# Sixteen of 44 weight cases of a down projection in a seven-product 2x2 scheme

## The chip, the cores and the metric

The kernel runs on one core of one Trainium2 chip. The metric is the device time of one execution, in microseconds (us), as the median of several runs. The engines are named as in the profile: PE is TensorE, DVE is VectorE, ACT is ScalarE, POOL is GpSimd, SP is the queue from which most transfers (DMAs) are issued.

## The reference

Two decoder layers over 256 tokens with a model width of 2048, each a mixer and a gated feed-forward network (FFN) with a causal convolution of width 3, and a final RMSNorm. The change concerns the second layer's FFN and the norm behind it.

```python
D_MODEL = 2048; SEQ = 256; DEPTH = 2; D_FF = 5632; CONV_W = 3; EPS = 1e-6

def conv_ffn(h, w_up, cw, cb, w_down):
    S = h.shape[1]
    a = h @ w_up                                   # 2048 -> 2 * 5632
    ap = jnp.pad(a, ((0, 0), (CONV_W - 1, 0), (0, 0)))
    c = sum(ap[:, k:k + S] * cw[k] for k in range(CONV_W)) + cb
    gate, val = c[..., :D_FF], c[..., D_FF:]
    return (jax.nn.silu(gate) * val) @ w_down      # 5632 -> 2048

def reference(x, mem, positions, ...):
    for l in range(DEPTH):
        ...
        x = x + jnp.concatenate([main, mo], axis=-1) @ w_out[l]
        x = x + conv_ffn(rmsnorm(x, g_ffn[l]), w_up[l], conv_w[l], conv_b[l], w_down[l])
    return rmsnorm(x, g_final)
```

## The kernel before

All data is fp32, and a product of fp32 accuracy is made of three matmuls. Each operand is split into a high part, which TensorE takes exactly, and the rest: `whi` is ACT's copy of a raw weight tile into the matmul's type, `wlo` is DVE's subtraction raw − `whi`. A product is then high × high + high × low + low × high. A raw tile is 128 x 1024 numbers (512 KB). There are four buffers for raw tiles, four for `whi` and five for `wlo`, so the loads and the splits run ahead of TensorE until one of these is used up.

The FFN takes the 5632 hidden columns in three parts of 4, 4 and 3 groups of 512 (`FF_GROUPS`). For each part there is an up stage: for each group a GEMM for the gate (`eg`) and one for the value (`ev`), both `gemm_fm`, feature-major, with matmuls of 256 columns; their results go through the convolution (`conv`: one operation on ACT, three on DVE), the gate through Silu, and gate times value, again split in two, lands in `h`. Then comes the part's down stage. In the first layer it is `gemm_fm` too. In the second layer it is token-major (`gemm_tm`, `mm_tm`): for each of four blocks j of 512 output columns, all blocks of 128 hidden columns (k blocks) of the part are multiplied for both blocks of 128 tokens (tb 0 and 1), with matmuls of 512 columns. The sum of a (j, tb) is one PSUM bank, which DVE adds to `xt`, the residual in token-major order (L1146).

In the last part the function `tokens` does the final norm beside it: for each (j, tb) ACT squares and sums (L1158), for j below 3 DVE multiplies by `gb`, the gain spread over the partitions (L1162), at j = 2 the three sums are reduced (L1165, L1166), and at j = 3 the scalar steps L1171 to L1178, the output scaling on ACT (L1182) and DVE (L1183, L1184) and the output transfers follow. `late=4` in the last j means that its last four chunks are done for tb 0 first and for tb 1 afterwards, the last chunk of tb 1 in two halves of 256 columns, and the order of PE, DVE and ACT is there as written. `gb` is loaded before this FFN.

Elsewhere a scheduler orders each engine's instructions, by its own estimates; `manual_schedule` fixes the written order within its scope.

Of the kernel before, what the change touches and what calls it, by code (L numbers as in the profile page):

```python
# [30 lines left out]
THETA = 10000.0  # L31
EPS = 1e-6
FF_GROUPS = (4, 4, 3)


def exact_pieces(value, bits, count):
# [33 lines left out]
class Kernel:  # L70
# [359 lines left out]

    def start(self):
        nc, t, tc = self.nc, self.t, self.tc
        self.x = self.ap.tile([P, NB, S], F32, name="xT")
        self.xhl = self.halves()
        mhl = self.ap.tile([P, NB, 512], F32R, tag="big", name=self.uid("memhl"))
        self.kT = [pool.tile([P, MH, S], F32, name=self.uid("kT")) for pool in (self.mk, self.cp)]
        self.mv = [pool.tile([P, 2, MW], F32, name=self.uid("mv")) for pool in (self.mk, self.cp)]
# [156 lines left out]
    def three(self, o, w, x, start, stop):  # L594
        mm, (wh, wl), (xh, xl) = self.nc.tensor.matmul, w, x
        mm(o, wh, xh, start=start, stop=False)  # L596
        mm(o, wh, xl, start=False, stop=False)  # L597
        mm(o, wl, xh, start=False, stop=stop)  # L598

    def memory_split(self, l, h, q, keys, rest):  # L600
        i, v = h % 2, self.mv[l][:, :, h * P : (h + 1) * P]
# [88 lines left out]
                done()  # L690


    def ffn(self, l, after=None, to_tokens=None, tokens=None):
        nc, t = self.nc, self.t
        rb = self.tmp(self.cp, [P, S], "rbc", 2)
# [3 lines left out]
        with self.tc.tile_pool(name=self.uid("ff"), bufs=1) as fp:  # L699
            g0 = 0  # L700
            for part, ng in enumerate(FF_GROUPS):
                h = self.ap.tile([P, NB, 512], F32R, tag="big", name=self.uid("h"))

                def conv(b, acc):
                    a = self.scaled(self.tmp(fp, [P, S], "a", 2), acc, rb)
# [4 lines left out]
                    nc.vector.scalar_tensor_tensor(c[:, 2:], a[:, : S - 2], w(0), c[:, 2:], ALU.mult, ALU.add)  # L710
                    return c

                for g in range(g0, g0 + ng):
                    gate = self.tmp(fp, [P, 4, S], "gate", 2)

                    def eg(b, acc):
                        c = conv(4 * g + b, acc)
                        nc.scalar.activation(gate[:, b, :], c, AF.Silu)

                    def ev(b, acc):  # L720
                        c = conv(FB + 4 * g + b, acc)
                        hv = self.tmp(fp, [P, S], "hv", 2)
                        nc.vector.tensor_tensor(hv, gate[:, b, :], c, ALU.mult)
                        self.split(h[:, 4 * (g - g0) + b, :], hv)

                    ks = list(range(NB))
                    turns = to_tokens if to_tokens is not None and g == 1 else {}
                    self.gemm_fm(self.rows(up, g * 512, 512), ks, 4, lambda k: xhl[k], eg, hooks=first if g == 0 else {})
                    self.gemm_fm(self.rows(up, FF + g * 512, 512), ks, 4, lambda k: xhl[k], ev, hooks=turns)
                last = part == len(FF_GROUPS) - 1  # L730
                if last and l == 0:
                    self.new_hl()
                dn = down[g0 * 512 : (g0 + ng) * 512]
                for j in range(4):
# [12 lines left out]
                    self.gemm_fm(src, list(range(4 * ng)), 4, lambda k: h[:, k, :], ed)  # L747
                g0 += ng


    def x_rstd(self):
# [363 lines left out]
    def run(self):  # L1115
        nc, tc, t = self.nc, self.tc, self.t
        self.constants()
        with tc.tile_pool(name="mk", bufs=1) as self.mk:
            self.start()
            self.layer_a()  # L1120
        self.ffn(0, lambda j: self.next_operand(j, None))
        self.layer_b()
        with tc.tile_pool(name="fin", bufs=1) as fin:

            xt = fin.tile([P, 2, D], F32, name="xt")
            gb = fin.tile([P, D], F32, name="gb")
            sums = fin.tile([P, 2, 5], F32, name="fsums")
            part = fin.tile([P, 2], F32, name="fpart")
            r = fin.tile([P, 2], F32, name="froot")
            q = fin.tile([P, 2], F32, name="fq")  # L1130
            v = fin.tile([P, 2], F32, name="fv")
            nc.sync.dma_start(out=gb, in_=t["g_final"].rearrange("(o d) -> o d", o=1).to_broadcast([P, D]))

            def turn(r):
                xs = self.tmp(fin, [P, 2, NB, 32], "xs", 2)
                ins = nc.vector.transpose(out=xs, in_=self.x.rearrange("p k (a r j) -> p a k r j", a=2, j=32)[:, :, :, r, :])
                tc.keep_in_program_order(ins)
                o = xt[32 * r : 32 * (r + 1)].rearrange("j a (k q i) -> j q (a k) i", q=4, i=32)
                for q in range(4):
                    nc.sync.dma_start(out=o[:, q], in_=xs[32 * q : 32 * (q + 1)].rearrange("j a k i -> j (a k) i"))  # L1140

            def tokens(j, tb, acc, last, half=None):
                c0, n = (0, 512) if half is None else (256 * half, 256)
                c = slice(j * 512 + c0, j * 512 + c0 + n)
                o = xt[:, tb, c]
                add = lambda o, a: nc.vector.tensor_tensor(o, a, o, ALU.add)  # L1146
                add(o, acc[:, c0 : c0 + n])
                if not last:
                    return
                junk = self.tmp(fin, [P, 512], "fjunk", 2)  # L1150
                one = lambda x: x[:, tb : tb + 1]
                if half == 1:

                    nc.vector.tensor_tensor_reduce(
                        out=junk[:, :n], in0=o, in1=o, scale=-0.5 / D, scalar=one(part), op0=ALU.mult, op1=ALU.add, accum_out=one(v)
                    )
                else:
                    nc.scalar.activation(junk[:, :n], o, AF.Square, accum_out=sums[:, tb, j : j + 1])  # L1158
                if half == 0:
                    add(xt[:, tb, j * 512 + 256 : (j + 1) * 512], acc[:, 256:])  # L1160
                if j < 3:
                    nc.vector.tensor_tensor(o, o, gb[:, c], ALU.mult)  # L1162
                if j == 2:

                    nc.vector.tensor_reduce(one(part), sums[:, tb, 0:3], AX.X, ALU.add)  # L1165
                    nc.vector.tensor_scalar(one(part), one(part), -0.5 / D, -0.5 * EPS, ALU.mult, ALU.add)  # L1166
                    nc.scalar.activation(one(r), one(part), AF.Sqrt, scale=-2.0)
                if j == 3:
                    if half != 1:
                        total = one(part) if half == 0 else one(v)  # L1170
                        nc.vector.tensor_scalar(total, sums[:, tb, 3:4], -0.5 / D, one(part), ALU.mult, ALU.add)  # L1171
                    if half == 0:
                        return

                    nc.scalar.activation(one(r), one(v), AF.Sqrt, scale=-2.0)
                    nc.vector.reciprocal(one(r), one(r))
                    nc.vector.scalar_tensor_tensor(one(q), one(r), one(r), one(v), ALU.mult, ALU.mult)
                    nc.vector.scalar_tensor_tensor(one(r), one(q), 1.5, one(r), ALU.add, ALU.mult)  # L1178

                    y, rows = xt[:, tb, :], slice(tb * P, (tb + 1) * P)  # L1180
                    for a in (0, 1024):
                        nc.scalar.activation(y[:, a : a + 512], y[:, a : a + 512], AF.Copy, scale=one(r))  # L1182
                    nc.vector.tensor_scalar(y[:, 512:1024], y[:, 512:1024], one(r), None, ALU.mult)  # L1183
                    nc.vector.scalar_tensor_tensor(y[:, 1536:], y[:, 1536:], one(r), gb[:, 1536:], ALU.mult, ALU.mult)  # L1184
                    nc.sync.dma_start(out=self.out[0, rows, :1024], in_=y[:, :1024])
                    (nc.scalar if tb else nc.sync).dma_start(out=self.out[0, rows, 1024:], in_=y[:, 1024:])

            turns = {2 * r: [lambda r=r: turn(r)] for r in range(4)}
            self.ffn(1, to_tokens=turns, tokens=tokens)


INV_FREQ = [float(1.0 / (THETA ** (2.0 * i / ROPE))) for i in range(HALF)]
# [23 lines left out]
```

## Time and profile before

| | |
|---|---|
| median of 3 runs | 2051.38 us (2051.24 to 2051.41) |
| the profiled execution | 2050.37 us, span 2048.6 us, granted clock 0.999 |
| PE busy | 2038.7 us, 16274 instructions |
| DVE busy | 1411.5 us, 2138 instructions |
| ACT busy | 1079.5 us, 1565 instructions |
| second layer's down stages | 1496.4 to 1583.4, 1757.6 to 1844.5 and 1975.2 to 2040.5 us |
| tail | 2040.5 to 2048.6 us |

The span is what the profiler records between the first and the last instruction; 1.8 us of the profiled execution's time lie around it. Busy times are sums over listed durations. Matmuls are pipelined, so the listed time of one is longer than the distance between two. In the rows that follow, "x" counts instructions, "<-" stands between an output and its inputs, and square brackets hold the idle time before an instruction and what ended it. In the windows table PEclk is the granted TensorE clock as a share of full speed and the number behind it the busy share of the DMA engines.

### The profile page before, as it was taken

The numbers are of one execution on the slowest core, as the hardware profiler recorded it, in microseconds if no ns is written. First come the engines' busy times: TensorE is split into PE (matmuls) and PEld (weight loads), VectorE is DVE, ScalarE is ACT, GpSimd is POOL, SyncE is SP. The second block draws the span as 40 slices with busy tenths as digits, with TensorE's granted clock in tenths as the row PEclk, the third lists the DMA queues.
The fourth block names the chain that finished last, engine by engine and source line by source line (L and its number), as shares of the span: only waits on it lengthen the run. The fifth ranks groups of instructions, "written<-read, shape, count | busy, mean of one in ns | idle before, by whom it ended". The sixth has DMA issues, their size and how long they took to land.

```text
span 2048.6 us, 39833 instructions
## 1 busy us (share of the span) xinstructions
PE 2038.7 (100%) x16274; PEld 1972.0 (96%) x16274; DVE 1411.5 (69%) x2138; ACT 1079.5 (53%) x1565; POOL 142.5 (7%) x200
## 2 busy tenths in 40 slices
PE   9999999999999999999999999999999999999998
PEld 8989999999999999999999999999988999889996
DVE  6866767767656766557788786777765667646765
ACT  6754744555435555345555575455543555435554
POOL 0000013000000000000043241400000000000000
PEclk9999999999999999999999999999999999999999
DMA  8776566666666666666665635568666666666664
GB/s 252 233 216 182 165 195 189 194 195 195 195 193 190 196 195 195 195 193 191 196 195 176 186 121 175 184 201 232 198 192 191 198 193 195 193 191 194 198 182 154
DMA packets 244796, 394.66 MB, mean 193 GB/s; under 512 B 53823, under 2 KB 61317, under 8 KB 244485
## 3 DMA queue, kind: packets, MB, share of 16 engines
q1 hardware_dynamic: 244420, 391.58, 64.2%
q8 instruction: 127, 2.08, 0.4%
q10 hardware_dynamic: 192, 0.54, 0.1%
q14 instruction: 57, 0.46, 0.1%
HBM read 387.88 MB, written 2.10 MB: 190 GB/s over the span
## 4 chain that ended last, share of the span: by engine, by line
PE 99%; ACT 0%; DVE 0%; DMA 0%; issue 0%; ACTq 0%
PE ps L152 26%; PE ps L153 26%; PE ps L155 26%; PE ps L184 6%; PE ps L185 6%; PE ps L186 6%; PE ps L518 1%; PE ps L597 0%; PE ps L598 0%; PE ps L596 0%; PE ps L1025 0%; PE ps L814 0%; PE ps L401 0%; PE ps L1053 0%; PE ps L639 0%; DMA graw<-in_g_mem 0%
## 5 line engine op out<-in xcount | busy, mean ns | idle before, releaser
L114 DVE TENSOR_TENSOR wlo<-raw,whi 128x1024 fp32r<-128x1024 f32 x660 | 818.4, 1243 | 517.4 <-ACT whi L113 511.5
L113 ACT ACTIVATE whi<-raw 128x1024 fp32r<-128x1024 f32 x660 | 700.4, 1062 | 845.1 <-PE ps L153 620.2
L152 PE MATMUL ps<-xhl,whi 128*128 128x256 f32 x3264 | 762.7, 277 | 0.0
L153 PE MATMUL ps<-xhl,whi 128*128 128x256 f32 x3264 | 761.0, 276 | 0.0
L153 PEld LDWEIGHTS ps<-xhl,whi 128*128 128x128 f32 x3264 | 612.7, 188 | 0.3
L152 PEld LDWEIGHTS ps<-xhl,whi 128*128 128x128 f32 x3264 | 612.7, 188 | 0.3
L155 PE MATMUL ps<-xhl,wlo 128*128 128x256 f32 x3264 | 436.5, 276 | 0.0
L155 PEld LDWEIGHTS ps<-xhl,wlo 128*128 128x128 f32 x3264 | 400.3, 188 | 0.0
L152 PE MATMUL ps<-h,whi 128*128 128x256 f32 x704 | 163.6, 276 | 0.0
L153 PE MATMUL ps<-h,whi 128*128 128x256 f32 x704 | 163.6, 276 | 0.0
L185 PE MATMUL ps<-wlo,h 128*128 128x512 f32 x354 | 137.2, 388 | 0.0
L184 PE MATMUL ps<-whi,h 128*128 128x512 f32 x354 | 136.8, 388 | 0.0
L186 PE MATMUL ps<-whi,h 128*128 128x512 f32 x354 | 136.8, 388 | 0.0
L153 PEld LDWEIGHTS ps<-h,whi 128*128 128x128 f32 x704 | 131.9, 188 | 0.0
L152 PEld LDWEIGHTS ps<-h,whi 128*128 128x128 f32 x704 | 131.8, 188 | 0.0
L152 PE MATMUL ps<-mainhl,whi 128*128 128x256 f32 x512 | 119.6, 277 | 0.0
L153 PE MATMUL ps<-mainhl,whi 128*128 128x256 f32 x512 | 119.3, 276 | 0.0
L708 ACT ACTIVATE c<-a,cT 128x256 f32<-128x256 f32 x176 | 99.3, 589 | 0.4 <-DVE a L232 0.3
L153 PEld LDWEIGHTS ps<-mainhl,whi 128*128 128x128 f32 x512 | 96.0, 188 | 0.0
L152 PEld LDWEIGHTS ps<-mainhl,whi 128*128 128x128 f32 x512 | 95.9, 188 | 0.0
L155 PE MATMUL ps<-h,wlo 128*128 128x256 f32 x704 | 94.1, 276 | 0.0
L232 DVE TENSOR_TENSOR a<-ps,rbc 128x256 f32<-128x256 f32 x176 | 69.9, 418 | 25.0 <-PE ps L155 24.9
(316 smaller groups left out, 2251.3 us busy)
## 6 DMA issues: line engine op xcount, KB each, us to landing
raw<-in_w_ffn_up SPq DMA_DIRECT2D x352, 512.0 KB, 4.3
raw<-in_w_ffn_down SPq DMA_DIRECT2D x176, 512.0 KB, 4.6
raw<-in_w_out SPq DMA_DIRECT2D x64, 512.0 KB, 4.5
raw<-in_w_in_a SPq DMA_DIRECT2D x56, 512.0 KB, 4.2
raw<-in_w_mem_kv SPq DMA_DIRECT2D x31, 512.0 KB, 4.3
raw<-in_w_in_b SPq DMA_DIRECT2D x16, 512.0 KB, 4.3
raw<-in_w_kv_a SPq DMA_DIRECT2D x9, 512.0 KB, 5.0
raw<-in_w_uq SPq DMA_DIRECT2D x12, 384.0 KB, 3.1
```

Of the source, the lines that this page charges most:

```text
L113: nc.scalar.activation(hi[:, :n], raw[:, :n], AF.Copy)
L114: nc.vector.tensor_tensor(lo[:, :n], raw[:, :n], hi[:, :n].bitcast(F32), ALU.subtract)
L152: mm(acc[:, :S], wh, x[:, :S], start=first, stop=False)
L153: mm(acc[:, :S], wh, x[:, S:], start=False, stop=False)
L155: mm(acc[:, :S], wl, x[:, :S], start=False, stop=last)
L184: mm(acc, xh, wh, start=first, stop=False)
L185: mm(acc, xh, wl, start=False, stop=False)
L186: mm(acc, xl, wh, start=False, stop=last)
L232: self.nc.vector.tensor_tensor(out, acc[:, :S], r, ALU.mult)
L518: nc.tensor.matmul(acc[:, :S], w[:, o : o + P], x, start=k == 0 and n == 0, stop=k == NB - 1 and n == 2)
L708: nc.scalar.activation(c, a, AF.Identity, scale=w(2), bias=w(3))
```

## The change

Only the second layer's down stages and the final norm are changed in substance. A part's down stage now has two phases of 1024 output columns each. A phase goes over pairs of k blocks; one pair by one phase is a case, two k blocks by two column blocks. There are 22 pairs, so 44 cases. A plain case is what it was: per token block and column block two products, 24 matmuls of 512 columns. A fast case sees the tokens (2 blocks) by k (2 blocks) times k by columns (2 blocks) as a 2x2 by 2x2 product and uses seven products in place of eight, 21 matmuls. Which pairs are fast, and the order of pairs in a phase, is in the table `FF_FAST`: three of eight pairs in the parts of four groups, two of six in the last, in both phases: 6 + 6 + 4 = 16 cases.

The right-hand sums of a fast case come from DVE in `fast_pair`: four sums of 512 columns (`xs`), and the splits of `y`, `x`'s left half (`we`), `t13` and `t24`: three `whi`/`wlo` of 1024 and one of 512. The left-hand sums are made once per pair in `ev` (`quarters`, tile `src`), by DVE, split on ACT and DVE.

A phase uses eight PSUM banks: `e00`, `e01`, `e10`, `e11` for the four output blocks, and `m1`, `m5`, `m6`, `m7` for products that more than one output needs. After the phase's last fast case `between` copies the four m banks to `staged` on ACT, and `combine` adds them to `xt` in six DVE operations. In the first two parts `combine` is put into the next part's first gate GEMM (`deferred`). In the last part the first phase's runs at the eviction of `e00`, the second's right after `between`. The evictions and the norm are now in `Tokens.evict`. The last phase has `late=2`: of its last two cases tb 1 is left to the end.

`gb` is now loaded at the start of the last part's down stage, into the SBUF of half of the FFN's input (tag `xhl0`), and `staged` into that of the residual. The raw loads of a down stage are 128 rows of 1024 columns in place of two blocks of 512. Hidden blocks that do not fit into `h` beside the sums go to other tiles (`place`). `three` swaps its second and third matmul. In `Tokens.evict` the output of columns 0 to 1023 is sent in two pieces.

```diff
 FF_GROUPS = (4, 4, 3)
+FF_FAST = {
+    4: ((2, 3, 4), ((0, 1, 2, 5, 3, 6, 4, 7), (2, 0, 3, 1, 4, 5, 6, 7))),
+    3: ((1, 2), ((0, 1, 3, 2, 4, 5), (1, 0, 2, 3, 4, 5))),
+}
...
+    def fast_pair(self, raws, pool):
...
+        b21, b22 = parts(y)
+        one = self.tmp(pool, [P, 1040], "we", 1, F32R)[:, :1024]
+        nc.scalar.activation(one[:, left], x[:, left], AF.Copy)
+        tt(one[:, right], x[:, left], one[:, left].bitcast(F32), ALU.subtract)
+        b11 = one[:, left], one[:, right]
+        t13, t24 = sums
+        tt(t13[:, left], x[:, left], x[:, right], ALU.add)
+        tt(t13[:, right], x[:, right], y[:, right], ALU.add)
+        t1, t3 = parts(t13)
+        tt(t24[:, left], t13[:, left], y[:, right], ALU.add)
+        tt(t24[:, right], t24[:, left], y[:, left], ALU.add)
+        t2, t4 = parts(t24)
+        return b21, b22, b11, t1, t3, t4, t2
...
+    def down_phase(self, dn, col, order, fast, lhs, rhs, pool, between, evict, late=0):
...
+            if k in fast:
+                names7 = "e00", "e01", "m1", "m5", "m7", "e10", "m6"
+                for name, q, w in zip(names7, (1, 6, 0, 4, 3, 2, 5), self.fast_pair(raws, pool)):
+                    three(name, rhs(k, q), w)
+                if k == last_fast:
+                    between([acc[m] for m in names[0]])
...
+        with self.tc.manual_schedule(engines={ET.PE, ET.DVE, ET.Activation}):
+            for half in range(2):
+                evict(0, half, acc[f"e0{half}"])
+            for k, ws in kept:
+                plain(k, ws, 1, 0)
+            evict(1, 0, acc["e10"])
...
-                    if tokens is not None:
-                        self.gemm_tm(
-                            src, 4 * ng, 512, lambda k: h[:, k, :], lambda tb, acc, i=None: tokens(j, tb, acc, last, i), late=4 if last and j == 3 else 0
-                        )
-                        continue
...
+    def between(self, accs):
+        for i, acc in enumerate(accs):
+            self.nc.scalar.activation(self.staged[:, self.ph, i, :], acc, AF.Copy)
+        if self.last and self.ph:
+            self.combine(1)
+        else:
+            self.waiting.append(self.ph)
+
+    def combine(self, ph):
+        xt, m = self.xt, self.staged[:, ph]
...
+        tt(m[:, 2], m[:, 2], m[:, 0], ALU.subtract)
+        tt(m[:, 3], m[:, 3], m[:, 2], ALU.add)
+        tt(xt[:, 0, n1], xt[:, 0, n1], m[:, 0], ALU.add)
+        tt(xt[:, 1, n1], xt[:, 1, n1], m[:, 3], ALU.subtract)
+        tt(xt[:, :, n2], xt[:, :, n2], m[:, 1:2].to_broadcast([P, 2, 512]), ALU.add)
+        tt(xt[:, :, n2], xt[:, :, n2], m[:, 2:4], ALU.add)
```

The order of instructions shows two places. The first is DVE in the last part's down stage, where one set of output columns is finished and the next begun. Before, two banks (`ps_23953`, `ps_23954`) are evicted between splits:

```order
L114 TENSOR_TENSOR wlo_24093<-raw_24091,whi_24092 128x1024
L114 TENSOR_TENSOR wlo_24111<-raw_24109,whi_24110 128x1024
L1146 TENSOR_TENSOR xt<-ps_23953,xt 128x512
L1146 TENSOR_TENSOR xt<-ps_23954,xt 128x512
L114 TENSOR_TENSOR wlo_24129<-raw_24127,whi_24128 128x1024
L1162 TENSOR_TENSOR xt<-xt,gb 128x512 x2
L114 TENSOR_TENSOR wlo_24147<-raw_24145,whi_24146 128x1024
```

Now, from the first eviction (`e00` of the first phase, `ps_24020`) to the third (L1359 is the eviction, L1340 `combine`, L725 to L729 the sums of the second fast case, L703 and L716 splits):

```order
L1359 TENSOR_TENSOR xt<-ps_24020,xt 128x512
L1340 TENSOR_TENSOR staged_24017<-staged_24017 128x512
L725 TENSOR_TENSOR xs_24384<-raw_24380 128x512
L716 TENSOR_TENSOR wlo_24320<-xs_24303,whi_24319 128x1024
L1340 TENSOR_TENSOR staged_24017<-staged_24017 128x512
L1340 TENSOR_TENSOR xt<-xt,staged_24017 128x512
L726 TENSOR_TENSOR xs_24384<-raw_24380,raw_24382 128x512
L703 TENSOR_TENSOR wlo_24349<-raw_24344,whi_24348 128x1024
L728 TENSOR_TENSOR xs_24385<-xs_24384,raw_24382 128x512
L722 TENSOR_TENSOR we_24390<-raw_24380,we_24390 128x512
L1340 TENSOR_TENSOR xt<-xt,staged_24017 128x512
L1340 TENSOR_TENSOR xt<-xt,staged_24017 128x2x512
```

Between the first and the next eviction there now stand the first phase's `combine`, two splits and the sums of the second fast case; the evictions of the other three banks follow after three more splits.

The second place is DVE at the end of the program. Before, tb 0's last block (`ps_24195`) is finished up to its scaling, then come the two halves of tb 1's (`ps_24196`, `ps_24328`):

```order
L1146 TENSOR_TENSOR xt<-ps_24195,xt 128x512
L1171 TENSOR_SCALAR fv<-fsums,fpart 128x1
L1176 RECIPROCAL froot<-froot 128x1
L1177 SCALAR_TENSOR_TENSOR fq<-froot,fv 128x1
L1178 SCALAR_TENSOR_TENSOR froot<-fq,froot 128x1
L1183 TENSOR_SCALAR xt<-xt,froot 128x512
L1184 SCALAR_TENSOR_TENSOR xt<-xt,froot,gb 128x512
L1146 TENSOR_TENSOR xt<-ps_24196,xt 128x256 x2
L1171 TENSOR_SCALAR fpart<-fsums,fpart 128x1
L1146 TENSOR_TENSOR xt<-ps_24328,xt 128x256
```

Now `e00` (`ps_24294`) and `e01` (`ps_24295`) stand there for tb 0, and `e10` (`ps_24296`) for tb 1:

```order
L1359 TENSOR_TENSOR xt<-ps_24294,xt 128x512
L1379 TENSOR_TENSOR xt<-xt,gb 128x512
L1381 TENSOR_REDUCE fpart<-fsums 128x1
L1382 TENSOR_SCALAR fpart<-fpart 128x1
L1359 TENSOR_TENSOR xt<-ps_24295,xt 128x512
L1387 TENSOR_SCALAR fv<-fsums,fpart 128x1
L1391 RECIPROCAL froot<-froot 128x1
L1392 SCALAR_TENSOR_TENSOR fq<-froot,fv 128x1
L1393 SCALAR_TENSOR_TENSOR froot<-fq,froot 128x1
L1397 TENSOR_SCALAR xt<-xt,froot 128x512
L1398 SCALAR_TENSOR_TENSOR xt<-xt,froot,gb 128x512
L1359 TENSOR_TENSOR xt<-ps_24296,xt 128x512
```

and after these `e10`'s own steps, before `e11` (`ps_24297`, and `ps_24569` for its last quarter):

```order
L1379 TENSOR_TENSOR xt<-xt,gb 128x512
L1381 TENSOR_REDUCE fpart<-fsums 128x1
L1382 TENSOR_SCALAR fpart<-fpart 128x1
L1359 TENSOR_TENSOR xt<-ps_24297,xt 128x256 x2
L1387 TENSOR_SCALAR fpart<-fsums,fpart 128x1
L1359 TENSOR_TENSOR xt<-ps_24569,xt 128x256
```

The block of columns 1024 to 1535 is thus finished together with the last block, for both tb, and no longer a block earlier. On ACT the same happens with the squares, and the load of the table for the square root stands between the two of tb 0:

```order
L1375 ACTIVATE fjunk_24523,fsums<-xt 128x512
L1383 ACT_TABLE_LOAD
L1383 ACTIVATE froot<-fpart 128x1
L1375 ACTIVATE fjunk_24530,fsums<-xt 128x512
L1390 ACTIVATE froot<-fv 128x1
L1396 ACTIVATE xt<-xt,froot 128x512 x2
```

It moves from beside the splits, where it is before, to behind the first Square of the end.

More of the change, by code (lines that the diff above doesn't have):

```diff
@@ L690, in w_out, with plain_pair, parts @@
                 done()
+    def plain_pair(self, raws):
+        nc, out = self.nc, []
+        for raw in raws:
+            hi, lo = self.split_tile("whi", True), self.split_tile("wlo", True)
+            nc.scalar.activation(hi, raw, AF.Copy)
+            nc.vector.tensor_tensor(lo, raw, hi.bitcast(F32), ALU.subtract)
+            out.append((hi, lo))
+        return out
+    def fast_pair(self, raws, pool):
+        nc, tt = self.nc, self.nc.vector.tensor_tensor
+        left, right = slice(0, 512), slice(512, 1024)
+        x, y = raws
+        sums = [self.tmp(pool, [P, 1024], "xs", 2) for _ in range(2)]
+        def parts(w):
+            hi, lo = self.split_tile("whi", True), self.split_tile("wlo", True)
+            nc.scalar.activation(hi, w, AF.Copy)
+            tt(lo, w, hi.bitcast(F32), ALU.subtract)
+            return [(hi[:, c], lo[:, c]) for c in (left, right)]
+        b21, b22 = parts(y)
[11 more added lines that the diff above has]
+        return b21, b22, b11, t1, t3, t4, t2
@@ L729, in ffn @@
-                    self.gemm_fm(self.rows(up, FF + g * 512, 512), ks, 4, lambda k: xhl[k], ev, hooks=turns)
-                last = part == len(FF_GROUPS) - 1
+                        tt = nc.vector.tensor_tensor
+                        n = 4 * (g - g0) + b
+                        if n // 2 not in fast:
+                            hv = self.tmp(fp, [P, S], "hv", 2)
+                            tt(hv, gate[:, b, :], c, ALU.mult)
+                            self.split(block(n), hv)
+                            return
@@ new lines, in ffn @@
+                    ks = list(range(NB))
+                    hooks_g, hooks_v = dict(first) if g == 0 else {}, {}
+                    if to_tokens is not None and g == 1:
+                        hooks_v = to_tokens
+                    if tokens is not None and part and g == g0:
+                        hooks_g = tokens.deferred()
+                    self.gemm_fm(self.rows(up, g * 512, 512), ks, 4, lambda k: xhl[k], eg, hooks=hooks_g)
+                    self.gemm_fm(self.rows(up, FF + g * 512, 512), ks, 4, lambda k: xhl[k], ev, hooks=hooks_v)
@@ L745, in ed @@
                             after(4 * j + b)
[L747 to L748 removed]
+                    self.gemm_fm(src, list(range(4 * ng)), 4, block, ed)
     def x_rstd(self):
@@ L1123, in run @@
         with tc.tile_pool(name="fin", bufs=1) as fin:
[L1125 to L1186, printed above, removed]
```

209 lines of the change are left out of this document (196 added, 13 removed).

## The prediction

> **What bounds the kernel now.** I read the page first: busy time by engine, then the chain that ended last.
>
> ```profile
> PE 2038.7 (100%) x16274; PEld 1972.0 (96%) x16274; DVE 1411.5 (69%) x2138; ACT 1079.5 (53%) x1565; POOL 142.5 (7%) x200
> ...
> PE 99%; ACT 0%; DVE 0%; DMA 0%; issue 0%; ACTq 0%
> ```
>
> TensorE is busy the whole span, and the chain of waits names it for 99%. So time can be won by fewer matmuls, as long as nothing else makes PE wait. The table of windows over the last FFN says what room the other engines have: the two down stages of four groups, the second part's up stage between them, the last down stage up to its last matmul, and the tail.
>
> ```profile
> core 0: us, PE busy (x) PEld busy (x) DVE busy (x) ACT busy (x) POOL busy (x), PEclk, DMA share, GB/s
> 1496.40:1583.40 87.00, 87.00 (x386) 72.01 (x385) 49.56 (x58) 36.37 (x40) 0.00 (x0) 1.00 0.63 192
> 1583.40:1757.60 174.20, 174.20 (x1538) 174.20 (x1537) 119.38 (x176) 91.67 (x121) 0.00 (x0) 1.00 0.67 194
> 1757.60:1844.50 86.90, 86.90 (x385) 71.91 (x385) 49.46 (x58) 36.33 (x40) 0.00 (x0) 1.00 0.63 193
> 1975.20:2040.50 65.30, 65.30 (x295) 54.17 (x293) 42.74 (x65) 32.19 (x50) 0.00 (x0) 1.00 0.49 152
> 2040.50:2048.60 8.10, 0.09 (x1) 0.00 (x0) 2.89 (x10) 1.91 (x5) 0.00 (x0) 0.83 0.51 203
> ```
>
> PE is at 100% at full clock in all three down stages. DVE has 37 us free in each of the first two and 23 in the third; DMA is busy for 0.63 of the time at most. After the last matmul 8.1 us remain. The waits view says why DVE idles:
>
> ```profile
> ACT whi L113 <- PE ps L153: 620.2, 430, 3.3
> DVE wlo L114 <- ACT whi L113: 511.5, 410, 3.9
> ACT whi L113 <- PE ps L186: 138.4, 84, 3.9
> ```
>
> The split runs ahead until its buffers are full: ACT waits for PE to free a `whi`, DVE waits for ACT. PE is not kept waiting by either.
>
> **The gain.** The timeline of PE gives the pitch of matmuls, which is shorter than the listed time of one.
>
> ```profile
> 2036.05 0.39 PE L186 MATMUL ps<-whi,h 128*128 128x512 f32 x1
> ...
> 2038.32 0.39 PE L184 MATMUL ps<-whi,h 128*128 128x512 f32 x1
> ...
> 2039.11 0.28 PE L185 MATMUL ps<-wlo,h 128*128 128x256 f32 x1
> ...
> 2040.31 0.28 PE L186 MATMUL ps<-whi,h 128*128 128x256 f32 x1
> ```
>
> Ten steps of 512 columns take 2.27 us, so 0.227 each; ten of 256 columns take 1.20. A plain case is 24 matmuls, 5.44 us; a fast one 21, 4.76. Sixteen fast cases save 48 × 0.227 = **10.9 us**, and the instruction order has exactly 48 matmuls fewer. That the change does not do what it says is thereby out.
>
> **What DVE gets to do.** Pitches again from the timeline, all of instructions that follow without waiting:
>
> ```profile
> 1496.64 1.23 DVE L114 TENSOR_TENSOR wlo<-raw,whi 128x1024 fp32r<-128x1024 f32 x1
> 1497.78 0.88 DVE L709 SCALAR_TENSOR_TENSOR c<-a,cT,c 128x255 f32<-128x255 f32 x2
> ...
> 1508.45 1.23 DVE L114 TENSOR_TENSOR wlo<-raw,whi 128x1024 fp32r<-128x1024 f32 x1 [0.82 <-ACT whi L113]
> 1509.59 0.42 DVE L241 TENSOR_TENSOR h<-hv,h 128x256 fp32r<-128x256 f32 x1
> ...
> 2026.47 0.69 DVE L1162 TENSOR_TENSOR xt<-xt,gb 128x512 f32<-128x512 f32 x1
> 2027.07 0.15 DVE L1165 TENSOR_REDUCE fpart<-fsums 128x1 f32<-128x3 f32 x1
> ```
>
> A 1024-wide operation takes 1.14 us to the next start (1.23 listed), a 512-wide one 0.60 (0.69 listed). A plain case is two splits, 2.28 us. A fast one is three 1024-wide splits, one 512-wide and four 512-wide sums: 3 × 1.14 + 5 × 0.60 = 6.42. `combine` is four 512-wide and two 1024-wide, 4.7. From 1496.64 to 1510.0 the convolution that hangs over from the up stage takes about 6.9 us beside the splits (13.4 less five splits, 5.7, and 0.8 of idle time). At most four splits (4.6 us; there are four `whi` buffers) are done before a down stage begins.
>
> Parts 0 and 1, first phase (three fast cases, five plain): 6.9 + 19.3 + 11.4 − 4.6 = 33.0 us of DVE in 3 × 4.76 + 5 × 5.44 = 41.5 of PE. DVE ends ahead, by the buffers no more than one fast case (6.4). The second phase to its third fast case: 4 × 0.60 for the evictions, 19.3 and 4.6, less 6.4, so 19.9 against 25.2. No shortage. But all eight accumulators are in use, so the next phase's products need banks whose evictions stand in DVE's queue among the sums of a fast case: I take one 512-wide operation of delay, 0.6 us each, **1.2 us** for both (0 if the banks are freed in time; up to 3.5 if a 1024- and a 512-wide one stand ahead each time).
>
> Part 2, first phase (two fast, four plain): 6.9 + 12.8 + 9.1 − 4.6 = 24.2 against 31.3; ahead by one fast case again. Its second phase begins with fast, plain, fast, 15.0 us of PE. DVE has evictions 2.4, the first phase's `combine` 4.7 (not deferred here, there is no later up stage), the multiplications by `gb` 2.4, and the three cases 15.1: 24.6 − 6.4 = 18.2. It is 3.2 us short. The product into the bank of `m1` must also await its copy on ACT; the nearest row, a 512-wide Square, lists 0.63, and part of it coincides, so 0.4. **3.6 us** together (1 if more is done ahead, 7 if what is done ahead is only two splits). Behind that, three plain cases (16.3 us of PE against 6.8 + 4.7 of DVE) catch up.
>
> [...]
>
> **The tail.** In before, the first 128 tokens (tb 0) are summed up well before the end; the timeline of DVE and ACT:
>
> ```profile
> 2028.08 1.28 ACT L1167 ACT_TABLE_LOAD   x1
> 2029.38 0.30 ACT L1167 ACTIVATE froot<-fpart 128x1 f32<-128x1 f32 x2
> 2035.12 0.69 DVE L1146 TENSOR_TENSOR xt<-ps,xt 128x512 f32<-128x512 f32 x1 [3.07 <-PE ps L186]
> 2035.90 0.63 ACT L1158 ACTIVATE fjunk<-xt 128x512 f32<-128x512 f32 x1 [5.12 <-DVE xt L1146]
> 2036.66 0.21 DVE L1171 TENSOR_SCALAR fv<-fsums,fpart 128x1 f32<-128x1 f32 x1 [0.85 <-ACT fjunk L1158]
> 2037.79 0.49 DVE L1183 TENSOR_SCALAR xt<-xt,froot 128x512 f32<-128x512 f32 x1
> 2038.19 0.75 DVE L1184 SCALAR_TENSOR_TENSOR xt<-xt,froot,gb 128x512 f32<-128x512 f32 x1
> 2039.91 0.76 DVE L1146 TENSOR_TENSOR xt<-ps,xt 128x256 f32<-128x256 f32 x2 [0.97 <-PE ps L186]
> 2040.91 0.21 DVE L1171 TENSOR_SCALAR fpart<-fsums,fpart 128x1 f32<-128x1 f32 x1 [0.25 <-ACT fjunk L1158]
> 2041.04 0.41 DVE L1146 TENSOR_TENSOR xt<-ps,xt 128x256 f32<-128x256 f32 x1
> ```
>
> PE's last matmul starts at 2040.31, so its slot ends at E = 2040.43. The last add starts at 2041.04, E + 0.61, and from it to the end of the span are 7.56 us.
>
> Afterwards three accumulators (tb 0, both halves, and tb 1's first) finish together, with 10 matmuls of 512 and 12 of 256 behind the first of them: its last matmul starts 11 × 0.227 + 12 × 0.12 = 3.93 before E. An add starts 0.44 after such a start (0.39 listed, 0.05 to the add), so at A = E − 3.49. DVE's order is then fixed. From A: Square 0.78; ACT's table load, which in before lay beside matmuls, stands behind it (Square 0.63 and accumulator read to 1.50) and ends at 2.80; the sqrt after it to 3.0; only then the Square of the second half; 0.76 on, the scalar step at 3.8; the output scaling 1.13 later at 4.9, its second operation at 5.3, 0.75 long. So tb 1's first half is added at 6.1; with 0.78 to its Square and 0.76 to its reduction 7.6; two 256-wide adds at 7.8; 1.00 to the scalar step and 0.13 to the last add, as at 2039.91 to 2041.04: 8.9. That is E + 5.4 against E + 0.61: **+4.8 us** (4.2 if the table is loaded early in part, 5.6 if every DVE step takes its listed time). What comes after the last add is unchanged.
>
> **What is hidden.** The left-hand sums of a fast pair cost about 1.3 us of DVE more in an up stage, and the deferred `combine` 4.7 twice; in the up stage from 1583.4 DVE has 55 us free in 174: cost 0, some 2 us if one landed on a full stretch. The 1 MB load of `gb` goes into SP's queue ahead of the raw loads of the second pair; it is released 96 matmuls (11 us) before the down stage. A raw load of half its size lands in 4.6 us,
>
> ```profile
> raw<-in_w_ffn_down SPq DMA_DIRECT2D x176, 512.0 KB, 4.6
> ```
>
> so at twice that, 9.2, it is done before the stage begins: 0, and up to 4.6 if that cover is gone and a raw load of the second pair stands behind it.
>
> **Sum.** −10.9 + 1.2 + 3.6 + 4.8 = −1.3. The profiled execution took 2050.37 us (span 2048.6 and 1.8 around it), so 2049.1; its median of runs is 1.0 higher, 2051.38, so **2050.1 us**. The forecast's own range is 2047.4 to 2054.5: PE waits from 2.5 to 8.5 with a tail of 4.8 to 5.6.
>
> **Rivals.** First: PE never waits, since the split runs 37 us in 87 ahead. For it speaks that no wait of PE shows in the down stages now; against it the 18.2 against 15.0 us. Then −10.9 + 4.8 = −6.1: 2045.3, faster.
>
> Second, on the other side: DVE becomes the bound because its operations cost their listed times, in the second phase of part 2 above all. A fast case is 3 × 1.23 + 5 × 0.69 = 7.1, a plain one 2.5, `combine` 5.2. Part 2's start of the second phase is then 2.8 + 5.2 + 2.8 + 16.7 = 27.5 less 4 ahead, 23.5 against 15.0: 8.5 us, and 0.4 for the bank; parts 0 and 1 with a slack of under 1 us lose 1.5 each at the phase change; the tail is 5.6. −10.9 + 8.9 + 3.0 + 5.6 = +6.6: 2058.0, slower. It decides from 10.2 us of PE waits on. For it speaks that sums are chained and each split waits for ACT; against it the pitches.
>
> Third: the tail stays as short as now, since tb 0 is finished beside matmuls. Then −10.9 + 4.8 = −6.1 with the waits: 2045.3. Against it stands the order, in which DVE takes tb 0 first.
>
> **Chances.** A measurement of this kernel can tell about 0.2%, 4.1 us, from no change. The forecast 0.58, PE never waiting 0.18, DVE as the bound 0.19, the short tail 0.05. Of the first and third, 0.20 lies more than 4.1 us below, and 0.02 of the forecast's lower edge; of the second 0.17 lies more than 4.1 above, and 0.03 of the forecast's upper edge. That makes faster 0.22, slower 0.20 and same 0.58. With a tenth left out on each side the range runs from 2045.9, near the first rival, to 2057.0, near the second.
>
> **What would show it.** Matmuls 48 fewer; PE gaps of some 4 us early in part 2's second phase, released by DVE splits and ACT copies; gaps under 1 us at the phase changes of parts 0 and 1; the last add 5 to 6 us behind the last matmul instead of 0.6, and about 13 us from the last matmul to the end. Wrong would be gaps of several us within phases of parts 0 and 1, PE at 100% through part 2, or a last add within 2 us of the last matmul.

## The result, and the profile after

The changed kernel takes 2057.98 us (median of six runs, 2055.74 to 2061.93), the kernel before 2051.15 in the same sessions. The ratio is 1.0040, with a 95% interval of 1.0029 to 1.0051: slower by 6 to 10 us. The forecast was 2050.1, its range ended at 2057.0. The profiled execution took 2055.74 us, with a span of 2054.0: 5.4 above the span before.

The page: busy times by engine, and the shares of the chain that ended last.

```profile
PE 2033.3 (99%) x16226; PEld 1962.6 (96%) x16226; DVE 1508.9 (73%) x2286; ACT 1115.4 (54%) x1613; POOL 142.0 (7%) x200
...
PE 90%; DVE 5%; DMA 3%; ACT 1%; issue 1%; DVEq 0%; ACTq 0%; SPq 0%
```

There are 48 matmuls fewer. The chain, 99% PE before, now runs 5% through DVE and 3% through transfers, all of them loads of `w_ffn_down`. The windows of the three down stages (the third in four pieces) and the end:

```profile
core 0: us, PE busy (x) PEld busy (x) DVE busy (x) ACT busy (x) POOL busy (x), PEclk, DMA share, GB/s
1496.90:1583.30 86.40, 84.45 (x368) 68.34 (x367) 71.89 (x92) 47.73 (x59) 0.00 (x0) 1.00 0.59 191
1757.40:1843.00 85.60, 84.44 (x369) 68.38 (x368) 71.94 (x92) 47.99 (x59) 0.00 (x0) 1.00 0.58 192
1973.50:2009.00 35.50, 35.50 (x158) 29.11 (x156) 34.33 (x52) 23.64 (x34) 0.00 (x0) 1.00 0.52 176
2009.00:2014.00 5.00, 3.68 (x16) 2.67 (x16) 5.00 (x7) 1.32 (x2) 0.00 (x0) 1.00 0.52 173
2014.00:2021.30 7.30, 6.61 (x28) 4.87 (x27) 6.87 (x9) 3.23 (x6) 0.00 (x0) 1.00 0.55 170
2021.30:2040.30 19.00, 18.67 (x87) 14.96 (x85) 16.07 (x21) 10.78 (x18) 0.00 (x0) 1.00 0.18 56
2040.30:2054.00 13.70, 0.12 (x2) 0.00 (x0) 6.80 (x21) 4.76 (x13) 0.00 (x0) 0.64 0.40 153
```

Parts 0 and 1 take 86.4 and 85.6 us, where the 384 matmuls of before (87.07 at full pitch) less 18 would be 83.0. DVE is busy 72 of 86 us there, so its work alone does not fill the stage. In part 2 DVE has 34.3 busy us out of 35.5 up to 2009 and all of the next 5, while PE stands still for 1.3. The end is 13.7 us where it was 8.1.

### The profile page after: what moved, and what is told of

Its sections match the earlier page's. It is cut to its first block, busy times and chain, and to the rows that moved or that the text cites. A ratio compares the mean times of both kernels' runs of the same rounds, so it can differ in the third digit from the quotient of the medians.

```text
span 2054.0 us, 39946 instructions
## 1 busy us (share of the span) xinstructions
PE 2033.3 (99%) x16226; PEld 1962.6 (96%) x16226; DVE 1508.9 (73%) x2286; ACT 1115.4 (54%) x1613; POOL 142.0 (7%) x200
## 4 chain that ended last, share of the span: by engine, by line
PE 90%; DVE 5%; DMA 3%; ACT 1%; issue 1%; DVEq 0%; ACTq 0%; SPq 0%
PE ps L156 25%; PE ps L157 25%; PE ps L159 25%; DMA raw<-in_w_ffn_down 3%; PE ps L188 2%; PE ps L190 2%; PE ps L189 2%; PE ps L752 1%; PE ps L753 1%; PE ps L751 1%; DVE wlo L703 1%; PE ps L523 1%; DVE wlo L716 1%; DVE xs L728 0%; DVE xt L1359 0%
## 5 line engine op out<-in xcount | busy, mean ns | idle before, releaser
L118 DVE TENSOR_TENSOR wlo<-raw,whi 128x1024 fp32r<-128x1024 f32 x572 | 710.3, 1245 | 392.5 <-ACT whi L117 387.8
L117 ACT ACTIVATE whi<-raw 128x1024 fp32r<-128x1024 f32 x572 | 606.5, 1062 | 703.1 <-PE ps L157 591.4
L752 PE MATMUL ps<-wlo,h 128*128 128x512 f32 (+1 forms) x226 | 88.3, 391 | 1.9 <-DVE wlo L703 1.9
L753 PE MATMUL ps<-whi,h 128*128 128x512 f32 (+1 forms) x226 | 87.5, 387 | 0.0
L122 ACT ACTIVATE whi<-raw,gT 128x512 fp32r<-128x512 f32 x96 | 63.9, 716 | 42.2 <-PE ps L157 21.4
```

Of the source, the lines that this page charges most:

```text
L117: nc.scalar.activation(hi[:, :n], raw[:, :n], AF.Copy)
L118: nc.vector.tensor_tensor(lo[:, :n], raw[:, :n], hi[:, :n].bitcast(F32), ALU.subtract)
L122: nc.scalar.activation(hi[:, s], raw[:, s], AF.Copy, scale=gains[k])
L752: mm(o, xh, wl, start=False, stop=False)
L753: mm(o, xl, wh, start=False, stop=stop)
```

## What DVE waits for in parts 0 and 1

The timeline of PE at the phase change of part 0:

```profile
1541.15 0.39 PE L751 MATMUL ps<-we,h 128*128 128x512 f32 x1
1542.79 0.50 PE L751 MATMUL ps<-whi,h 128*128 128x512 f32 x1 [1.24 <-DVE xt L1359]
...
1547.52 0.50 PE L752 MATMUL ps<-wlo,h 128*128 128x512 f32 x1 [0.53 <-DVE wlo L703]
```

PE waits for a bank that DVE's eviction (L1359) must free. The idle time in brackets counts from the listed end of the matmul before, 0.16 us behind its slot at full pitch (0.39 listed, 0.23 apart), and the starts behind a wait follow 0.34 and 0.24 apart. So the waits listed in part 0 add up to 1.9 us, and the delay of the starts to 3.4. The timeline of DVE says why the eviction is late:

```profile
1534.02 1.22 DVE L703 TENSOR_TENSOR wlo<-raw,whi 128x1024 fp32r<-128x1024 f32 x1
...
1536.29 1.22 DVE L716 TENSOR_TENSOR wlo<-xs,whi 128x1024 fp32r<-128x1024 f32 x1
1540.30 0.69 DVE L725 TENSOR_TENSOR xs<-raw 128x512 f32<-128x512 f32 x1 [2.79 <-DMA raw<-in_w_ffn_down]
1540.91 1.22 DVE L716 TENSOR_TENSOR wlo<-xs,whi 128x1024 fp32r<-128x1024 f32 x1
1542.05 0.68 DVE L1359 TENSOR_TENSOR xt<-ps,xt 128x512 f32<-128x512 f32 x1
```

DVE was idle for 2.79 us at the first sum of the next fast case, whose raw tile had not landed, and the eviction stood behind that sum. The waits view counts such waits:

```profile
ACT we L721 <- DMA raw<-in_w_ffn_down: 19.8, 12, 3.0
DVE xs L725 <- DMA raw<-in_w_ffn_down: 12.3, 12, 2.8
```

Twelve of the 16 fast cases begin with DVE waiting for a transfer. A fast case needs its first raw tile until its second sum and the other until its last sum and its split of `y`; a plain case needs each only for one split. With four raw tiles a load is issued only when DVE is done with a tile. The load awaited at 1540.30 was issued by SP when the plain split of 1534.02, which stood in DVE's queue among the sums of a fast case, had ended (1535.24):

```profile
1535.26 0.33 SPq L766 DMA_DIRECT2D raw<-in_w_ffn_down  x1
```

It landed 5.0 us later; the median of these loads is 4.4. That became theory A: the raw tiles are held too long. Theory B was the prediction's second rival: DVE's own work at listed times.

## Experiments: the raw tiles

Six raw tiles in place of four: the two more are the `gate` tiles of the up stage, which lie idle in most of a down stage.

```diff
-                raw = self.wp.tile([P, 1024], F32, tag="raw", name=self.uid("raw"), bufs=4)
+                if n % 3 == 2:
+                    raw = self.tmp(self.fp, [P, 4, S], "gate", 2).rearrange("p b s -> p (b s)")
+                else:
+                    raw = self.wp.tile([P, 1024], F32, tag="raw", name=self.uid("raw"), bufs=4)
```

> Every third pair of the down stages takes its two raw tiles from the two gate buffers of the up stage, which lie idle there: six raw buffers in place of four. Theory A (a fast case holds both its raw tiles through its whole chain of sums, so the next loads are issued late and DVE stands still for a transfer, with the evictions behind it): the PE gaps of 3.2 and 2.4 us in parts 0 and 1 fall to 1 or less each, those of part 2 from 4.0 to 2 or 3, the time falls by 4 to 6 us against the changed kernel, to 2052 to 2054, and the runs lie within 2 us instead of 6. Theory B (the work of DVE itself, chained sums at their listed times): the gaps stay, the time stays within 1 us of the changed kernel.

It took 2059.37 us, no gain. The gap at the phase change was gone, but part 0 got others; PE and DVE, early in part 0:

```profile
1507.38 0.73 PE L751 MATMUL ps<-whi,h 128*128 128x512 f32 x2 [0.70 <-ACT whi L715]
```

```profile
1506.21 0.69 DVE L726 TENSOR_TENSOR xs<-gate,gate 128x512 f32<-128x512 f32 x1 [2.81 <-DMA gate<-in_w_ffn_down]
```

The load into a gate tile was issued at 1502.53, when the last convolution had done with the tile, and part 2 took 70.8 us, with a wait of 2.21 us and a lowered clock behind it (matmuls 0.43 us apart). So this did not decide. The next used gate tiles from the fourth pair on:

```diff
-                if n % 3 == 2:
+                at = n + len(order) * (col // 1024)
+                if at and at % 3 == 0:
```

> Six raw buffers as before, but the two gate buffers are used first by the fourth pair of a part's down stage and by every third after it, when the last convolution no longer needs them (the earlier kernel with six used them for the third pair, whose load waited for the convolution). Theory A (raw buffers): no gap at the phase changes of parts 0 and 1 and none at their start, 1 us or less of PE waits in each (changed kernel: 3.2 and 2.4); part 2 keeps its waits and its slow clock, so 2 to 5 us below the changed kernel. Theory B (DVE's work): 2 to 3 us of waits stay in each of parts 0 and 1.

2061.05 us: still too early. A plain case waited for its gate tile 2.25 us in part 0 and 1.58 in part 1, and part 2 took 70.9 us, with a wait of 3.11.

To see parts 0 and 1 alone, part 2 was given back its old down stage and end:

```diff
-                fast, orders = FF_FAST[ng] if tokens is not None else ((), None)
+                fast, orders = FF_FAST[ng] if tokens is not None and not last else ((), None)
...
+                    if last:
+                        tokens.begin(0, True)
+                        for j in range(4):
...
+                            self.gemm_tm(src, 4 * ng, 512, block, et, late=4 if j == 3 else 0)
+                        continue
```

> Parts 0 and 1 as in the changed kernel (12 fast cases), part 2's down stage and the end as in the kernel before (four blocks of 512 columns, late=4, no fast case); gb still loads late. If the loss sits in part 2 and the end: 12 x 0.68 = 8.2 gained, 5.6 lost in the waits of parts 0 and 1, part 2 and the end at their old lengths: 2 to 3 us below the kernel before. If the fast cases lose wherever they are: at or above the kernel before.

2049.59 us, ratio 0.9998 (0.9989 to 1.0007). This lies between the two expectations. Of the 8.2 us won by 12 fast cases little is left: in the profile parts 0 and 1 lose 2.3 and 4.4 us to waits.

```profile
1495.70:1581.00 85.30, 84.17 (x368) 68.23 (x367) 71.81 (x92) 47.88 (x59) 0.00 (x0) 1.00 0.60 193
1755.10:1842.50 87.40, 84.44 (x369) 68.35 (x368) 71.92 (x92) 47.87 (x59) 0.00 (x0) 1.00 0.58 188
```

With the gate tiles of raw6b:

> The same with the six raw buffers of raw6b in parts 0 and 1. Theory A: 6 to 8 us below the kernel before. Theory B: 2 to 3 below, as without them.

2049.44 us, ratio 0.9995 (0.9986 to 1.0004): neither theory's number, since the fourth pair waits for the gate tiles here too (1.19 us in part 0; 2.19 in part 1, with a lowered clock behind, matmuls 0.42 us apart). The last of these uses the gate tiles only when the convolution is over:

```diff
-                if at and at % 3 == 0:
+                if at > 4 and at % 3 == 2:
```

> As part2old_raw6, but the two gate buffers are used from the sixth pair of a part on, when the last convolution is surely over. Theory A (raw buffers): neither the gaps at the phase change nor those of the two earlier kernels at the third and fourth pair; parts 0 and 1 within 1 us of 83.0 each (87.07 less 18 matmuls), so 6 to 8 us below the kernel before. Theory B (DVE's work): 85 to 87 each, at most 2 below the kernel before.

2045.10 us, ratio 0.9977 (0.9966 to 0.9987): 5 us below the kernel before and 13 below the changed one, 4.5 below the same kernel with four raw tiles. This version beats both kernels. But its windows, for parts 0 and 1, show 85.2 and 85.1 us, not 83; the time lies nearer to theory A's number, the lengths of the parts lie in theory B's range:

```profile
1496.60:1581.80 85.20, 83.60 (x368) 68.55 (x367) 72.51 (x93) 48.52 (x59) 0.00 (x0) 1.00 0.57 187
1755.90:1841.00 85.10, 83.59 (x368) 68.56 (x367) 71.71 (x92) 48.29 (x59) 0.00 (x0) 1.00 0.58 187
```

Its timeline of DVE at the phase change says what is left, the same wait in two smaller pieces (PE then waits a second time, 0.79 us, for ACT's `we`):

```profile
1537.30 0.69 DVE L725 TENSOR_TENSOR xs<-raw 128x512 f32<-128x512 f32 x1 [0.52 <-DMA raw<-in_w_ffn_down]
1539.53 0.69 DVE L726 TENSOR_TENSOR xs<-raw,raw 128x512 f32<-128x512 f32 x1 [1.53 <-DMA raw<-in_w_ffn_down]
1540.14 1.22 DVE L716 TENSOR_TENSOR wlo<-xs,whi 128x1024 fp32r<-128x1024 f32 x1
1541.27 0.69 DVE L1376 TENSOR_TENSOR xt<-ps,xt 128x512 f32<-128x512 f32 x1
```

Whether still more tiles would remove it was not tried. A change of tiles also lets the scheduler order things anew, so the 4.5 us are not the transfers' alone, and the two profiles show only 2.4 of them in parts 0 and 1.

What decides better is a comparison without a change of order. In five traces (`part2old`, and of runs that come below `tail`, `nocomb` and both profiles of the changed kernel) PE, DVE and ACT have the same order of instructions in parts 0 and 1, so DVE's own work is the same as well. Yet PE's waits range from 2.3 to 4.4 us a part. The three parts in which DVE waited least for raw tiles (5.4 to 5.7 us) have the smallest waits of PE (2.3 to 2.7), and the one in which it waited longest (7.5) has the largest; between these the order is loose, since 6.0 went with 4.3. With six tiles DVE waited 2.4 and 3.7 us and PE 2.2 and 2.1. So the raw tiles were a cause. One wait does not move with them: the one for `wlo` behind the evictions (1547.52 above) is 0.53 to 0.55 us in all ten parts. It comes from DVE's own order.

Theory B, that the operations cost their listed times, falls by the changed kernel's own timeline, since the operations of a fast case follow each other 0.60 to 0.61 apart, not 0.69:

```profile
1554.54 0.69 DVE L725 TENSOR_TENSOR xs<-raw 128x512 f32<-128x512 f32 x1 [1.82 <-DMA raw<-in_w_ffn_down]
1555.15 0.69 DVE L722 TENSOR_TENSOR we<-raw,we 128x512 fp32r<-128x512 f32 x1
1555.76 0.69 DVE L726 TENSOR_TENSOR xs<-raw,raw 128x512 f32<-128x512 f32 x1
1556.36 0.69 DVE L728 TENSOR_TENSOR xs<-xs,raw 128x512 f32<-128x512 f32 x1
```

## Experiments: part 2 and the clock

The runs of the changed kernel lie 6 us apart, those of the kernel before within 1.5. A second profile was taken for that.

> The changed kernel once more, for a second profile. Its first had no lowered clock in part 2 and was the fastest of its six runs (2055.74, median 2057.98). If a wait over 2 us with a lowered clock behind it makes the slower runs: a profile near the median shows one, as the kernels tail and raw6 did, with matmuls 0.43 us apart. If not: the difference is spread over many small waits, or lies at the start of the program.

Its execution took 2061.65 us, so it is not one near the median (2057.97 of five runs). The windows around the second phase's start, and PE there:

```profile
2009.00:2014.00 5.00, 3.13 (x14) 2.28 (x13) 5.00 (x8) 2.71 (x4) 0.00 (x0) 1.00 0.07 16
2014.00:2021.30 7.30, 6.61 (x18) 4.70 (x17) 6.89 (x8) 0.60 (x1) 0.00 (x0) 0.53 0.75 235
```

```profile
2012.80 0.50 PE L752 MATMUL ps<-wlo,h 128*128 128x512 f32 x1 [1.87 <-DVE wlo L703]
...
2016.59 0.63 PE L752 MATMUL ps<-wlo,h 128*128 128x512 f32 x1
2017.02 0.63 PE L753 MATMUL ps<-whi,h 128*128 128x512 f32 x1
```

Where the first profile has a wait of 0.64 us and a clock of 1.00, this one waits 1.87, and from 2014 to 2021 the granted clock is 0.53 and matmuls stand 0.43 apart: 18 in 7.3 us in place of 28. Part 2 is 70.4 us long from its first matmul to its last of 512 columns, 65.3 in the first profile. With DVE busy throughout, the DMA share from 2009 to 2014 is 0.07: no load is issued between 2005.4 and 2012.8, since SP waits for DVE to free a raw tile. DVE came to this stretch 3 us later than in the first profile, 0.9 of it because the stage began later, and after idle waits for transfers that the first has not or has shorter:

```profile
1998.99 0.69 DVE L725 TENSOR_TENSOR xs<-raw 128x512 f32<-128x512 f32 x1 [0.51 <-DMA raw<-in_w_ffn_down]
2002.27 0.69 DVE L726 TENSOR_TENSOR xs<-raw,raw 128x512 f32<-128x512 f32 x1 [0.85 <-DMA raw<-in_w_ffn_down]
2007.97 0.69 DVE L725 TENSOR_TENSOR xs<-raw 128x512 f32<-128x512 f32 x1 [0.34 <-DMA raw<-in_w_ffn_down]
2011.52 1.22 DVE L703 TENSOR_TENSOR wlo<-raw,whi 128x1024 fp32r<-128x1024 f32 x1
```

Of the eleven executions of the changed kernel the four above 2061 us have mean granted clocks of 0.996, 0.996, 0.996 and 0.998, the other seven 0.997 or 0.998. So the lowered clock goes with most of the long ones, not with each.

To test DVE's queue, the first phase's `combine` was left out in part 2:

```diff
         if self.ph == 0 and half == 0 and tb == 0:
-            for ph in self.waiting:
-                self.combine(ph)
             self.waiting = []
```

> The changed kernel without the combine of the first phase in part 2 (its six DVE operations, 4.7 us, are left out, so those products are missing from the output). If DVE's queue early in the second phase makes PE wait there: the waits near the start of that phase fall from 3 or more us to 1.5 or less, no single one over 1, the clock stays at 1.00, and the time falls by 3 to 5 us against the changed kernel, with less spread. If banks or ACT's copies do: no change of the waits, and the time stays within 1 us.

2055.06 us, 2.9 below the changed kernel. From 2009 to 2021.3 the waits are small and the clock is full:

```profile
2009.00:2021.30 12.30, 11.89 (x52) 9.31 (x51) 12.30 (x17) 7.88 (x12) 0.00 (x0) 1.00 0.50 160
```

Part 2 takes 62.8 us, 1.6 above what its matmuls need. So DVE's queue sets part 2, as forecast. The time fell by a little less than the 3 to 5 us expected, and the runs still lie 4.7 us apart; in this profile parts 0 and 1, which the edit does not touch, lose 4.3 and 3.6 us to waits, 2 us more than in the first profile.

## Experiments: the end

> No fast case at all, the phases of 1024 columns, the four banks, the late load of gb and the new end stay (no m banks, no combine). If only fast cases make PE wait: no gap in the down stages, 2051.2 + 5.6 for the end = about 2057, 1 below the changed kernel. If the phases themselves cost (four evictions at once, transfers of gb): above 2058.

The table `FF_FAST` without fast pairs: 2056.19 us, and no gap of PE in any down stage; all waits come from fast cases. It is 6.3 us above the kernel before, and its trace shows an end of 13.7 us as the only loss in these stages: a loss nearly as large as the changed kernel's is there without any fast case. What the fast cases save, they give back in waits. The end, first in allplain, then in the changed kernel:

```profile
2042.20:2055.90 13.70, 0.14 (x2) 0.00 (x0) 6.80 (x21) 4.78 (x13) 0.00 (x0) 0.66 0.40 153
```

```profile
2036.77 0.69 DVE L1359 TENSOR_TENSOR xt<-ps,xt 128x512 f32<-128x512 f32 x1 [1.22 <-PE ps L753]
2038.23 1.28 ACT L1383 ACT_TABLE_LOAD   x1
2038.25 0.69 DVE L1379 TENSOR_TENSOR xt<-xt,gb 128x512 f32<-128x512 f32 x1 [0.79 <-ACT fjunk L1375]
2040.58 0.21 DVE L1387 TENSOR_SCALAR fv<-fsums,fpart 128x1 f32<-128x1 f32 x1 [0.79 <-ACT fjunk L1375]
2042.78 0.68 DVE L1359 TENSOR_TENSOR xt<-ps,xt 128x512 f32<-128x512 f32 x1
2044.25 0.69 DVE L1379 TENSOR_TENSOR xt<-xt,gb 128x512 f32<-128x512 f32 x1 [0.79 <-ACT fjunk L1375]
2044.86 0.15 DVE L1381 TENSOR_REDUCE fpart<-fsums 128x1 f32<-128x3 f32 x1
2046.29 0.41 DVE L1359 TENSOR_TENSOR xt<-ps,xt 128x256 f32<-128x256 f32 x1
```

The chain is the forecast one: e00 at 2036.77, the table load behind its Square, e10 at 2042.78, the last add 9.5 us behind the first. Then the order of the accumulators was changed to e00, e10, e01, e11, each evicted when done:

```diff
-            for half in range(2):
-                evict(0, half, acc[f"e0{half}"])
-            for k, ws in kept:
-                plain(k, ws, 1, 0)
-            evict(1, 0, acc["e10"])
+            for tb in range(2):
+                for k, ws in kept:
+                    plain(k, ws, tb, 0)
+                evict(tb, 0, acc[f"e{tb}0"])
+            for k, ws in kept:
+                plain(k, ws, 0, 1)
+            evict(0, 1, acc["e01"])
```

> The four accumulators of the last phase are finished one after the other (e00, e10, e01, e11) for the last two cases, in place of e00 and e01 together; nothing else. If DVE's fixed order behind e00 sets the end: the stretch from the last matmul to the end falls from 13.7 us to about 9.5 and the time by about 4, to 2054. If something behind it sets the end (output transfers, ACT's scaling): under 1 us.

2059.39 us. The end did fall, to 10.0 us. But the order now needs the last pair's splits earlier, while DVE is still at `combine`, and PE waited 1.91 us for a `wlo`, besides 2.21 at the start of the phase, with a lowered clock behind each (matmuls 0.43 us apart). With six raw tiles besides:

> Both edits together. If the two losses are independent, as theory A and the order of the end have it, the gains add: 8 to 10 us below the changed kernel, 2048 to 2050, 1 to 3 us below the kernel before. By theory B only the end gains: 2054.

2059.34 us, for the reasons of both; the end is 10.0 us here too. Without fast cases the order could be tried by itself, first with e00 and e10 taken case by case ahead of the fixed order:

> No fast case, and the last two cases in the order e00 and e10 (case by case), then e01, then e11; the evictions in that order. If the order of the accumulators makes the end 13.7 us long: about 9.5 from the last matmul to the end, with no PE gap, so 4 us below the kernel without fast cases and 2 above the kernel before. If something else does: 13 to 14 us and no gain.

2055.66 us, an end of 13.8: the scheduler mixed e01's matmuls in, so e00 finished as late as before. Then the order of the kernel tail, without fast cases:

> No fast case; the last two cases in the order e00 (both cases), e10, e01, e11, all of it in the fixed order of PE. In the kernel allplain_tail2 the scheduler had mixed e01 in among e00 and e10, so that e00 still ended 3.5 us before the last matmul. Here e00 ends some 8 us before it. If the time of e00 and DVE's chain of 9.5 us behind it set the end: 8.5 to 9.5 us from the last matmul to the end instead of 13.7, 4 to 5 us below allplain, 1 to 2 above the kernel before. If not: 13 to 14 us.

2052.36 us, 3.8 below allplain; an end of 10.0 us, and PE lost 0.9 us ahead of it.

```profile
2040.50:2050.50 10.00, 0.15 (x2) 0.00 (x0) 4.57 (x14) 3.38 (x7) 0.00 (x0) 0.60 0.54 210
```

The order of the accumulators sets most of the change in the end, though 0.5 to 1.5 us more is left than expected, and 1.9 more than the 8.1 of the kernel before.

## Why the prediction was wrong

The time from the first to the last matmul of each stage (in part 2, to the last of 512 columns), against what its matmuls need at full pitch (83.0, 83.0 and 61.2 us), gives each term for the two profiles of the changed kernel, in us:

| term | forecast | first profile | second profile |
|---|---|---|---|
| 48 matmuls | −10.9 | −10.9 | −10.9 |
| waits in part 0 | 0.6 | 3.4 | 3.7 |
| waits in part 1 | 0.6 | 2.6 | 2.7 |
| waits and clock in part 2 | 3.6 | 4.1 | 9.1 |
| the end | 4.8 | 5.5 | 5.5 |
| start of the first down stage | 0 | 0.7 | 1.2 |
| sum, against the span before | −1.3 | +5.4 | +11.3 |

The last row but one is not put down to the change: over all kernels that stage began between 1494.9 and 1498.0 us, and what moves it was not looked into. The measured median lies between the two profiles, nearer to the first.

- **The gain** was right, and so was that nearly all of it would be given back; it was more than all.
- **Parts 0 and 1: the step that failed.** It found no shortage of DVE's work and let one operation, 0.6 us, stand ahead of an eviction at each phase change. A delay of that size by DVE's order is there (the constant wait for `wlo` behind the evictions, 0.7 us of PE's starts). But as limits to working ahead it counted the `whi` and `wlo` buffers and not the raw tiles, of which a fast case holds one until its last sum; that DVE itself stands still for a load, with an eviction behind it, was no term of the sum. Of transfers it looked at their share of time, 0.63 at most; what mattered was when a load could be issued. Measured were 6.0 and 6.4 us for 1.2. In the traces six raw tiles leave 4.4 of the 5.9 to 7.9 us that four have; how the rest divides between loads and DVE's order is open.
- **Part 2: mechanism right, price short.** DVE's queue of evictions, `combine`, gain and two fast cases was named, and `nocomb` bore it out. 4.1 us against 3.6 where the clock stayed up; with the clock down 9.1. The clock was left out of the prediction altogether.
- **The end: mechanism right, 0.7 us short.** Up to e10's add the steps came within 0.1 us of the forecast. But e10's reduction stands behind its multiplication by `gb`, which overwrites what Square reads and so starts 1.47 us after the add; from the add to the reduction that makes 2.1 us, not 1.54.
- **What was called hidden** was: the loads of `gb` and the left-hand sums show no wait of PE in the up stages.
- **The rivals.** The second gave 2058.0, 0.02 from the measured median, by a mechanism that does not hold: DVE's operations do not cost their listed times (0.60 apart for 0.69). Its place was right in part: it had 8.9 us in part 2, where 4.1 and 9.1 were measured, and 3.0 in parts 0 and 1, where it was 6.0 and 6.4. Its total was right by chance. PE never waiting, and a short end, were excluded by the trace.
- **The range.** By the prediction's own terms its lower end is 2047.8 us (2051.38 − 10.9 + 2.5 + 4.8), not 2047.4; nothing rests on the difference.

## What to carry to other kernels

When an operand is reused by more steps, ask of every buffer on its way how long it is now held, and price the load that waits for it: issue plus landing time, in front of everything that stands behind the waiting instruction on its engine. An engine at 83%, as DVE in part 0, with a queue in fixed order can still stop the one that bounds. And look at the end of the program first: here a reordered end cost 5.5 us, half of what 48 matmuls brought, and has nothing to do with them.

## What the runs showed of the hardware

In these runs some short waits of TensorE cost more than themselves. In the traces of these kernels, in the second layer's down stages, ten single waits were between 1.58 and 3.11 us; behind nine of them matmuls of 512 columns followed at 0.43 us in place of 0.23 for 2.5 to 7 us (the granted clock was 0.53 in the window behind the wait of 1.87). None of 1.31 us or less had that. One wait of 2.25 us passed without it, though a wait of 1.87 us (the second profile of the changed kernel) had it: the length of a wait did not settle it alone, and what did was not shown.
